# In a Mamba-2 and attention trunk, the convolved x of groups 1 to 7 is turned by VectorE in 32x32 blocks, and a DRAM scratch moves the blocks

## The chip, the cores and the metric

The kernel runs on one core of one Trainium2 chip. The metric is the device time of one launch, in microseconds; lower is better. The time before is the median of three runs, 1022.89 us (1022.04 to 1023.73).

A core has a matmul engine (TensorE, PE in the profile, with PEld for its weight loads), a vector engine (VectorE, DVE), an activation engine (ScalarE, ACT), GpSimd (POOL), and SyncE (SP), which here issues DMAs. Each engine runs its own queue of instructions in order and waits on semaphores for the others.

## What is computed

Two layers on x of 256 positions by 2048 features, float32. Layer one is a Mamba-2 SSD mixer, layer two attention in a sliding window; each is followed by a residual and a LayerNorm. The change lies in layer one. Cut to what matters, with 8 groups of 8 heads, 64 features in each head, and chunks of 128 positions:

```python
zxbcdt = x @ w_in
xbc = silu(causal_conv4(zxbcdt[..., D_INNER:D_INNER + CONV_DIM]) + conv_b)
xs, bm, cm = split(xbc)                      # xs: (256, 64 heads, 64)
x_c = xs * dt[..., None]                     # by chunk, group, head
cb = einsum("bcqgn,bcsgn->bgcqs", c_c, b_c)
y_diag = einsum("bgcqs,bgrcqs,bcsgrp->bcqgrp", cb, decay_in, x_c)
# plus the part that comes from the chunk before (y_off)
y = (y_diag + y_off) + xs * d_skip
y = y * silu(z);  y = y * rsqrt(mean(y**2) per group) * norm_w
h = y @ w_out
```

The sum over the positions s in `y_diag` needs x with positions on the partitions. The convolution works with positions along the free axis, so it leaves x the other way round: channels on the partitions. Between the two, x has to be turned.

## The kernel before

Every weight matrix comes in units of 128 x 2048 float32 (1 MB), each loaded by SP in two halves into `wr` buffers (L125, five buffers). ACT makes the rounded high half `wh` (L133) and DVE the remainder `wl` (L134); there are four slots of each. A product of full precision is three matmuls: high by high, low by high, high by low (`mac`, L195 to L197; `out_unit`, L255 to L257).

Layer one runs in 8 groups of 10 blocks. A block is one weight unit, 48 matmuls into one PSUM tile `mm` (four tiles). In groups 1 to 7 the order is B, C, four xs blocks, four z blocks (`BLOCKS`); group 0 has z first (`BLOCKS0`). After a B, C or xs block `conv_silu` empties `mm` on ACT (L357) and DVE (L359, three shifted terms) into a `cv` tile and ends with a tanh on ACT (L362) and a product on DVE (L363). After a z block, L428 and L429 do the gate. The output projection of group g-1 (`out_units`) is spread between the blocks of group g; L262 adds its result into the residual `xr`.

What else belongs to a group is placed by hand. `plan` holds, for a time counted in blocks (10 g + block), the functions that are traced after that block. For group g >= 2 the decay is loaded, summed and exponentiated first (`load_decay`, `sum_decay`, `exp_decay`), then come `cb` at 4, `tr` at 7 (`TR_AT`), `ymm` and four `gate` at 9 (`Y_AT`), and `norm` at 14. For group 0 `tr` is at 12 and `ymm` at 13, that is, inside group 1. The framework then sets each engine's queue from that order, its own estimate of when an instruction is ready and the buffers that are free, and puts in all waits. A tile's tag names the buffers that it takes turns in.

- `tr` (L453, L458): for a group, eight 128x128 transposes on PE against the identity into two PSUM tiles `ax`. DVE multiplies what came out by `dtx` (dt times a decay factor) into four tiles `xd`.
- `ymm` (L476): 32 matmuls, with `xd` as the stationary operand and the decay `e` as the moving one. DVE multiplies by `el` into `yz` (L481) and adds the skip term, which reads xs again (L487).
- `gate`: POOL multiplies by z (L492) and squares; ACT and DVE split the result into `yH` and `yL` (L506, L507) for the output projection.
- `make_dt` and `turn_dt`: once, ahead of the groups; `dtx` is made in the second (L345). The cumulated decay goes through a DRAM scratch `rscr` (stores at L327 and L330) and comes back, spread over all partitions, as `rb` (L374) and `el` (L387).

The four xs tiles of a group, the seven tiles of `make_dt` and the squares of `gate` take turns in seven buffers of 1 KB per partition with the tag `sm`.

Of the kernel before, what the change touches and what calls it, by code (L numbers as in the profile page):

```python
# [8 lines left out]
F32 = mybir.dt.float32  # L9
# [3 lines left out]
ALU = mybir.AluOpType  # L13
AX = mybir.AxisListType

P = 128
S = 256
D = 2048
KT = D // P
NG = 8  # L20
DI = 4096
KT2 = DI // P
NHD = 64
# [11 lines left out]

BLOCKS = list(range(10))
BLOCKS0 = [6, 7, 8, 9, 0, 1, 2, 3, 4, 5]
CB_AT, TR_AT, Y_AT, NSM = 4, 7, 9, 7
B_ORDER = [("q", 0), ("g", 0), ("q", 1), ("g", 1), ("o", 0), ("q", 2), ("g", 2), ("o", 1),
           ("q", 3), ("g", 3), ("o", 2), ("o", 3)]  # L40
ALPHA = (2.0 * 2) ** 0.25
# [16 lines left out]
def trunk(ctx: ExitStack, tc: tile.TileContext, A: dict, out: bass.AP, dbg=None):  # L58
    nc = tc.nc
# [12 lines left out]
    dram = pool("dram", space=bass.MemoryType.DRAM)  # L72
# [3 lines left out]
    def nm(s):  # L76
        uid[0] += 1
        return f"{s}_{uid[0]}"
# [8 lines left out]
    ident = cc[:, 0:128]  # L87
# [4 lines left out]
    pc = cst.tile([P, PC_END], F32, tag="pc", name="pc")  # L92
# [132 lines left out]
    ap = pool("ap", stack=w_stack)  # L225
# [66 lines left out]
        return pss  # L292


    dtx = ap.tile([P, 2, NHD], F32, tag="dtx", name="dtx")
    rtk = ap.tile([P, 2, 2 * NHD], F32, tag="rtk", name="rtk")
    rscr = dram.tile([P, S], F32, tag="rscr", name="rscr")

    def make_dt(ps):
        f = [ap.tile([P, S], F32, tag="sm", name=nm("f"), bufs=NSM) for _ in range(7)]  # L300
        u, e, rec, z, w, q, dt = [x[:] for x in f]
        nc.scalar.activation(u, ps[:, :S], AF.Identity, bias=pc[:, PC_DTB : PC_DTB + 1])
        nc.scalar.activation(e, u, AF.Abs)
        nc.scalar.activation(e, e, AF.Exp, scale=-1.0)
        aneg = ap.tile([P, 1], F32, tag="aneg", name="aneg")
        nc.scalar.activation(aneg[:], pc[:, PC_ALOG : PC_ALOG + 1], AF.Exp)
        nc.vector.tensor_scalar(aneg[:], aneg[:], -1.0, None, ALU.mult)
        nc.vector.tensor_scalar(rec, e, 2.0, None, ALU.add)
        nc.vector.reciprocal(rec, rec)
        nc.vector.tensor_tensor(z, e, rec, ALU.mult)  # L310
        nc.vector.tensor_tensor(w, z, z, ALU.mult)
        nc.vector.tensor_scalar(q, w, 1.0 / 15.0, None, ALU.mult)
        nc.vector.tensor_scalar(z, z, 2.0, None, ALU.mult)
        for d in (13.0, 11.0, 9.0, 7.0, 5.0, 3.0):
            nc.vector.scalar_tensor_tensor(q, q, 1.0 / d, w, ALU.add, ALU.mult)
        nc.vector.scalar_tensor_tensor(q, q, 1.0, z, ALU.add, ALU.mult)
        nc.vector.scalar_tensor_tensor(dt, u, 0.0, q, ALU.max, ALU.add)
        da, hi = e, rec
        nc.vector.tensor_scalar(da, dt, aneg[:], None, ALU.mult)
        nc.vector.tensor_scalar(hi, da, QUANT, None, ALU.add)  # L320
        nc.vector.tensor_scalar(hi, hi, QUANT, None, ALU.subtract)
        nc.vector.tensor_tensor(hi[64:128], da[64:128], hi[64:128], ALU.subtract)
        one = z
        nc.gpsimd.memset(one, 1.0)
        rc = w
        nc.vector.tensor_tensor_scan(rc, one, hi, 0.0, ALU.mult, ALU.add)
        nc.sync.dma_start(rscr[0:64, :], rc[:64])  # L327

        nc.scalar.activation(hi[64:128], rc[64:128], AF.Exp)
        nc.sync.dma_start(rscr[64:128, :], hi[64:128])  # L330
        return rc, dt, q

    def turn_dt(rc, dt, q):
        pt = ax_tile()
        for c in range(2):
            nc.tensor.transpose(pt[:, c * P : (c + 1) * P], rc[:, c * P : (c + 1) * P], ident)
            nc.tensor.transpose(
                pt[:, 256 + c * 64 : 320 + c * 64], dt[:64, c * P : (c + 1) * P], ident[:64, :64]
            )
        nc.scalar.copy(rtk[:], pt[:, :256].rearrange("p (c h) -> p c h", c=2))  # L340
        elo = q
        nc.scalar.activation(
            elo[:, :128].rearrange("p (c h) -> p c h", c=2), rtk[:, :, 64:128], AF.Exp, scale=-1.0
        )
        nc.vector.tensor_tensor(  # L345
            dtx[:], pt[:, 256:384].rearrange("p (c h) -> p c h", c=2),
            elo[:, :128].rearrange("p (c h) -> p c h", c=2), ALU.mult,
        )

    def conv_silu(ps, t, dst):  # L350
        def w(i):
            c = PC_CONV + t * 5 + i
            return pc[:, c : c + 1]

        a = ap.tile([P, S], F32, tag="cv", name=nm("cv"), bufs=3)
        with tc.high_priority(CPRI):
            nc.scalar.activation(a[:], ps[:, :S], AF.Identity, scale=w(3), bias=w(4))  # L357
            for sft in (1, 2, 3):
                nc.vector.scalar_tensor_tensor(  # L359
                    a[:, sft:], ps[:, : S - sft], w(3 - sft), a[:, sft:], ALU.mult, ALU.add  # L360
                )
        nc.scalar.activation(dst, a[:], AF.Tanh)  # L362
        nc.vector.scalar_tensor_tensor(dst, dst, 1.0, a[:], ALU.add, ALU.mult)  # L363
# [54 lines left out]
        conv_silu(ps, g * 6 + 1, gs[g].ct[:])  # L418

    def in_xs(g, i, ps):  # L420
        xs = ap.tile([P, S], F32, tag="sm", name=nm("xs"), bufs=NSM)
        conv_silu(ps, g * 6 + 2 + i, xs[:])
        gs[g].__dict__.setdefault("xs", {})[i] = xs

    def in_z(g, i, ps):
        z = ap.tile([P, S], F32, tag="zz", name=nm("z"), bufs=4)
# [16 lines left out]
            )  # L443

    def tr(g):
        st = gs[g]
        st.xd = {}
        for k in range(2):
            ps = ax_tile()
            for i in (2 * k, 2 * k + 1):  # L450
                for c in range(2):
                    o = (i % 2) * S + c * P
                    nc.tensor.transpose(ps[:, o : o + P], st.xs[i][:, c * P : (c + 1) * P], ident)  # L453
            for i in (2 * k, 2 * k + 1):
                o = (i % 2) * S
                xd = ap.tile([P, 2, 2, 64], F32, tag="xd", name=nm("xd"), bufs=4)
                hh = g * 8 + 2 * i
                nc.vector.tensor_tensor(  # L458
                    xd[:], ps[:, o : o + S].rearrange("p (c h d) -> p c h d", c=2, h=2),
                    dtx[:, :, hh : hh + 2].unsqueeze(3).to_broadcast([P, 2, 2, 64]), ALU.mult,  # L460
                )
                st.xd[i] = xd

    def ymm(g):
        st = gs[g]
        st.yz = ap.tile([P, 4, S], F32, tag="yz", name=nm("yz"), bufs=1)
        for k in range(2):
            ps = ax_tile()
            for i in (2 * k, 2 * k + 1):
                o = (i % 2) * S  # L470
                xd = st.xd[i]
                for c in range(2):
                    cols = slice(o + c * P, o + S)
                    for r in range(2):
                        e = es[g, i // 2][:, 2 * (i % 2) + r, :]
                        nc.tensor.matmul(  # L476
                            ps[64 * r : 64 * r + 64, cols], xd[:, c, r, :], e[:, 256:] if c else e[:, :256],
                            start=c == 0, stop=c == 1,
                        )
            two = slice(2 * k, 2 * k + 2)  # L480
            nc.vector.tensor_tensor(  # L481
                st.yz[:, two, :], ps[:].rearrange("p (i q) -> p i q", i=2), els[g][:, two, :], ALU.mult
            )
            for i in (2 * k, 2 * k + 1):
                col = PC_D + g * 4 + i
                v = st.yz[:, i, :]
                nc.vector.scalar_tensor_tensor(v, st.xs[i][:], pc[:, col : col + 1], v, ALU.mult, ALU.add)  # L487

    def gate(g, i):
        st = gs[g]  # L490
# [103 lines left out]
    def at(t, fn, *a):  # L594
        plan.setdefault(t, []).append((fn, *a))

    at(35, rotary)
    for g in range(NG):
        t = 10 * g
        if g == 0:  # L600
            at(TD, turn_dt, *dts)
            at(TS, load_decay, 0, 1)
            at(TS, load_low, 0)
            steps = TS
            pos = dict(cb=CB0, tr=12, y=13, norm=16)
        elif g == 1:
            at(10, load_decay, 1, 0)
            at(10, load_decay, 1, 1)
            at(13, load_low, 1)
            steps = 13  # L610
            pos = dict(cb=6, tr=TR_AT, y=Y_AT, norm=10 + CB_AT)
        else:
            at(t - 5, load_decay, g, 0)
            at(t - 5, load_decay, g, 1)
            at(t, load_low, g)
            steps = t - 1
            pos = dict(cb=CB_AT, tr=TR_AT, y=Y_AT, norm=10 + CB_AT)
        at(steps, sum_decay, g, 0)
        at(steps + 1, exp_decay, g, 0)
        at(steps + 1, sum_decay, g, 1)  # L620
        at(steps + 2, exp_decay, g, 1)
        at(t + pos["cb"], cb, g)
        at(t + pos["tr"], tr, g)
        at(t + pos["y"], ymm, g)
        for i in range(4):
            at(t + pos["y"], gate, g, i)
        at(t + pos["norm"], norm, g)
# [93 lines left out]
    for h in range(2):  # L721
        ps = mm_tile()
# [304 lines left out]
```

## Time and profile before

| | us |
|---|---|
| median of 3 runs | 1022.89 |
| lowest and highest run | 1022.04, 1023.73 |
| span of the profiled execution, first to last instruction | 1022.1 |
| PE busy in the span | 1001.7 |
| DVE busy | 774.2 |
| ACT busy | 562.8 |

For the profiled execution the page gives its span only; what lies around the span is seen from the runs, which are 0.0 to 1.6 us longer.

The page lists busy times by engine, the span in 40 slices (each digit a tenth of a slice), the DMA queues and the costliest groups of instructions. A group's row has the line, the engine, the operation, what it writes and reads, the shapes, the count, the busy time and the mean duration in ns, and after the bar the engine's idle time ahead of it, with the instruction that ended it. A row of a timeline begins with the start in us from the span's start and the duration in us; rows of the same kind in succession are merged, with their count. The windows view gives each engine's busy time in a stretch, the granted clock, the DMA share and GB/s. A row of the waits view names the waiting instruction, the one that it waited for, the time in us, the count and the longest wait.

### The profile page before, as it was taken

What the parts mean: (1) busy time and instruction counts of PE and PEld (TensorE: products, weight loads), DVE (VectorE), ACT (ScalarE), POOL (GpSimd) and SP (SyncE); (2) the same over time, 40 slices, a digit from 0 to 9 for tenths busy, and PEclk for the clock granted to TensorE, in tenths of its full rate; (3) what the DMA queues carried; (4) which work ended last, traced back from release to release, by engine and by line L of the source; (5) the groups of instructions that cost most, each with busy time, mean ns of one, the idle gap of its engine ahead of it and who ended that gap; (6) DMA issues with size and microseconds to landing.
All of it is one profiled execution on the core that took longest, in us unless ns stands there. A gap on an engine that the chain in (4) does not pass through costs nothing. (4 is left out here: it accounts for less than half of the span.)

```text
span 1022.1 us, 17627 instructions
## 1 busy us (share of the span) xinstructions
PE 1001.7 (98%) x7028; PEld 905.5 (89%) x7028; DVE 774.2 (76%) x1106; ACT 562.8 (55%) x924; POOL 89.8 (9%) x112
## 2 busy tenths in 40 slices
PE   7999999999999999999999999999999999999997
PEld 7999899999998998999999999868988879879975
DVE  6868887876886787696786787798577785785776
ACT  6585857637655655664663763535545453453642
POOL 0000303004003002100300300301000000000002
PEclk9999999999999999999999999999999999999999
DMA  8786676575666666656656556647655445545522
GB/s 308 249 299 246 204 245 195 171 233 169 211 218 191 218 195 204 205 188 202 208 179 218 156 190 210 227 146 232 197 167 169 156 140 183 173 140 183 194 96 82
DMA packets 57794, 199.31 MB, mean 195 GB/s; under 512 B 6304, under 2 KB 10672, under 8 KB 56944
## 3 DMA queue, kind: packets, MB, share of 16 engines
q1 hardware_dynamic: 56352, 192.14, 57.3%
q0 software_dynamic: 1072, 5.53, 1.5%
q8 instruction: 55, 0.90, 0.4%
q10 hardware_dynamic: 288, 0.52, 0.1%
q14 instruction: 27, 0.22, 0.1%
HBM read 195.93 MB, written 2.23 MB: 194 GB/s over the span
## 5 line engine op out<-in xcount | busy, mean ns | idle before, releaser
L134 DVE TENSOR_TENSOR wl<-wr,wh 128x1024 fp32r<-128x1024 f32 (+2 forms) x342 | 398.3, 1181 | 135.4 <-ACT wh L133 134.0
L133 ACT ACTIVATE wh<-wr 128x1024 fp32r<-128x1024 f32 (+2 forms) x342 | 337.4, 1011 | 238.9 <-PE mm L196 77.1
L195 PE MATMUL mm<-xH,wh 128*128 128x256 f32 x1296 | 361.2, 279 | 8.0 <-ACT wh L153 6.0
L197 PE MATMUL mm<-xH,wl 128*128 128x256 f32 x1296 | 359.8, 278 | 2.1 <-DVE wl L134 2.1
L196 PE MATMUL mm<-xL,wh 128*128 128x256 f32 x1296 | 360.1, 278 | 0.0
L195 PEld LDWEIGHTS mm<-xH,wh 128*128 128x128 f32 x1296 | 244.6, 189 | 10.2 <-ACT wh L153 6.3
L197 PEld LDWEIGHTS mm<-xH,wl 128*128 128x128 f32 x1296 | 244.5, 189 | 2.7 <-DVE wl L134 2.7
L196 PEld LDWEIGHTS mm<-xL,wh 128*128 128x128 f32 x1296 | 244.7, 189 | 1.1
L255 PE MATMUL mm<-wh,yH 128*128 128x512 f32 x256 | 101.4, 396 | 0.0
L256 PE MATMUL mm<-wh,yL 128*128 128x512 f32 x256 | 99.9, 390 | 0.0
L257 PE MATMUL mm<-wl,yH 128*128 128x512 f32 x256 | 99.7, 390 | 0.0
L492 POOL TENSOR_TENSOR yz<-yz,z 128x256 f32<-128x256 f32 x32 | 32.9, 1036 | 532.0 <-DVE yz L487 532.0
L195 PE MATMUL mm<-x1H,wh 128*128 128x256 f32 x256 | 71.9, 281 | 0.0
L197 PE MATMUL mm<-x1H,wl 128*128 128x256 f32 x256 | 71.0, 277 | 0.0
L196 PE MATMUL mm<-x1L,wh 128*128 128x256 f32 x256 | 71.0, 277 | 0.0
L359 DVE SCALAR_TENSOR_TENSOR cv<-mm,pc,cv 128x255 f32<-128x255 f32 x144 | 68.6, 476 | 1.4
L712 PE MATMUL mm<-wh,x1H 128*128 128x512 f32 x160 | 63.3, 396 | 0.0
L714 PE MATMUL mm<-wl,x1H 128*128 128x512 f32 x160 | 62.6, 392 | 0.3 <-DVE wl L134 0.2
L713 PE MATMUL mm<-wh,x1L 128*128 128x512 f32 x160 | 62.6, 391 | 0.2 <-DVE x1L L676 0.2
L255 PEld LDWEIGHTS mm<-wh,yH 128*128 128x128 f32 x256 | 48.1, 188 | 10.3 <-DVE z L429 1.0
L257 PEld LDWEIGHTS mm<-wl,yH 128*128 128x128 f32 x256 | 48.1, 188 | 10.2
L256 PEld LDWEIGHTS mm<-wh,yL 128*128 128x128 f32 x256 | 48.1, 188 | 9.0
(180 smaller groups left out, 1306.2 us busy)
## 6 DMA issues: line engine op xcount, KB each, us to landing
wr<-in_wa SPq DMA_DIRECT2D x158, 512.0 KB, 5.0
wr<-in_wo SPq DMA_DIRECT2D x64, 512.0 KB, 4.8
wr<-in_wq SPq DMA_DIRECT2D x32, 512.0 KB, 4.5
wr<-in_wg SPq DMA_DIRECT2D x32, 512.0 KB, 5.2
wr<-in_wb SPq DMA_DIRECT2D x32, 512.0 KB, 4.6
rb<-rscr SPq DMA_DIRECT2D x16, 512.0 KB, 5.4
el<-rscr SPq DMA_DIRECT2D x16, 256.0 KB, 4.8
wr<-in_wkv SPq DMA_DIRECT2D x8, 512.0 KB, 4.3
```

Of the source, the lines that this page charges most:

```text
L133: nc.scalar.activation(h[:, sl], raw, AF.Copy)
L134: nc.vector.tensor_tensor(l[:, sl], raw, h[:, sl].bitcast(F32), ALU.subtract)
L195: nc.tensor.matmul(ps, ah, bh, start=first, stop=False)
L196: nc.tensor.matmul(ps, ah, bl, start=False, stop=False)
L197: nc.tensor.matmul(ps, al, bh, start=False, stop=last)
L255: nc.tensor.matmul(ps[:], aH[:, k, hs], u.h[:, ks], start=k == 0, stop=False)
L256: nc.tensor.matmul(ps[:], aL[:, k, hs], u.h[:, ks], start=False, stop=False)
L257: nc.tensor.matmul(ps[:], aH[:, k, hs], u.l[:, ks], start=False, stop=k == 3)
L359: nc.vector.scalar_tensor_tensor(a[:, sft:], ps[:, : S - sft], w(3 - sft), a[:, sft:], ALU.mult, ALU.add)
L712: nc.tensor.matmul(ps[:], x1H[:, kk, hs], u.h[:, ks], start=kk == 0, stop=False)
L713: nc.tensor.matmul(ps[:], x1L[:, kk, hs], u.h[:, ks], start=False, stop=False)
L714: nc.tensor.matmul(ps[:], x1H[:, kk, hs], u.l[:, ks], start=False, stop=kk == KT - 1)
```

## The change

In groups 1 to 7 `tr` is replaced by three steps:

- `turn_blocks`, after block 5: two VectorE transposes, one for each chunk, turn every 32x32 block of the group's x in place of the whole 128x128. The result `zt` has the positions within a block of 32 on the partitions. Four stores on SP, one for each band of 32 partitions, write it to a DRAM scratch `zd` so that the blocks stand in the order that a whole transpose would give.
- `load_turned`, after block 6: one load on SP brings it back as `xt`, with all 128 positions on the partitions.
- `scale_x`, after block 8: two DVE multiplications by `dtx` of 512 columns each, from SBUF, give `xd`.

`ymm` stays after block 9. Group 0 keeps `tr` with PE and the identity.

Buffers change along with it. A group's four xs are one tile with the tag `xs` and one buffer; four of the seven tiles of `make_dt` use that buffer before. The tag `sm` goes from seven buffers to three. `xd` is one tile for a group, and `zt` and `xt` take turns with `yz` in its one buffer. `dtx` is laid out by group, and is written by two instructions in place of one.

```diff
-CB_AT, TR_AT, Y_AT, NSM = 4, 7, 9, 7
+CB_AT, ZT_AT, LD_AT, XD_AT, Y_AT, NSM = 4, 5, 6, 8, 9, 3
...
-    dtx = ap.tile([P, 2, NHD], F32, tag="dtx", name="dtx")
+    dtx = ap.tile([P, NG, 2, 8], F32, tag="dtx", name="dtx")
...
     def make_dt(ps):
-        f = [ap.tile([P, S], F32, tag="sm", name=nm("f"), bufs=NSM) for _ in range(7)]
-        u, e, rec, z, w, q, dt = [x[:] for x in f]
+        f = [ap.tile([P, S], F32, tag="sm", name=nm("f"), bufs=NSM) for _ in range(3)]
+        f4 = ap.tile([P, 4, S], F32, tag="xs", name=nm("f4"), bufs=1)
+        u, e, rec, z = [f4[:, i, :] for i in range(4)]
+        w, q, dt = [x[:] for x in f]
...
-        nc.vector.tensor_tensor(
-            dtx[:], pt[:, 256:384].rearrange("p (c h) -> p c h", c=2),
-            elo[:, :128].rearrange("p (c h) -> p c h", c=2), ALU.mult,
-        )
+        for c in range(2):
+            cols = slice(64 * c, 64 * c + 64)
+            nc.vector.tensor_tensor(
+                dtx[:, :, :, 4 * c : 4 * c + 4],
+                pt[:, 256:384][:, cols].rearrange("p (g i r) -> p g r i", i=4, r=2),
+                elo[:, cols].rearrange("p (g i r) -> p g r i", i=4, r=2), ALU.mult,
+            )
...
     def in_xs(g, i, ps):
-        xs = ap.tile([P, S], F32, tag="sm", name=nm("xs"), bufs=NSM)
-        conv_silu(ps, g * 6 + 2 + i, xs[:])
-        gs[g].__dict__.setdefault("xs", {})[i] = xs
+        if i == 0:
+            gs[g].xs = ap.tile([P, 4, S], F32, tag="xs", name=nm("xs"), bufs=1)
+        conv_silu(ps, g * 6 + 2 + i, gs[g].xs[:, i, :])
...
     def tr(g):
         st = gs[g]
-        st.xd = {}
+        st.xd = ap.tile([P, 8, 2, 64], F32, tag="xd", name=nm("xd"), bufs=1)
...
+    def turn_blocks(g):
+
+        st = gs[g]
+        zt = ap.tile([P, 4, 2, 4, 32], F32, tag="yz", name=nm("zt"), bufs=1)
+        xv = st.xs[:].rearrange("p i (c b t) -> p c b i t", c=2, b=4)
+        for c in range(2):
+            nc.vector.transpose(zt[:, :, c, :, :], xv[:, c, :, :, :])
+        st.zd = dram.tile([4, P, 256], F32, tag="zd", name=nm("zd"), bufs=2)
+        for a in range(4):
+            nc.sync.dma_start(
+                st.zd[a, :, :].rearrange("(b t) f -> t b f", b=4),
+                zt[32 * a : 32 * a + 32, :, :, :, :].rearrange("p b c i d -> p b (c i d)"),
+            )
+
+    def load_turned(g):
+        st = gs[g]
+        st.xt = ap.tile([P, 2, 2, 8, 32], F32, tag="yz", name=nm("xt"), bufs=1)
+        nc.sync.dma_start(st.xt[:].rearrange("p r a k d -> p (r a) (k d)"), st.zd[:].rearrange("a p f -> p a f"))
+
+    def scale_x(g):
+
+        st = gs[g]
+        st.xd = ap.tile([P, 8, 2, 64], F32, tag="xd", name=nm("xd"), bufs=1)
+        xv = st.xd[:].rearrange("p k r (a d) -> p r a k d", a=2)
+        for r in range(2):
+            nc.vector.tensor_tensor(
+                xv[:, r, :, :, :], st.xt[:, r, :, :, :],
+                dtx[:, g, r, :].unsqueeze(1).unsqueeze(3).to_broadcast([P, 2, 8, 32]), ALU.mult,
+            )
...
-                            ps[64 * r : 64 * r + 64, cols], xd[:, c, r, :], e[:, 256:] if c else e[:, :256],
+                            ps[64 * r : 64 * r + 64, cols], st.xd[:, 4 * c + i, r, :], e[:, 256:] if c else e[:, :256],
...
-        at(t + pos["tr"], tr, g)
+        if g == 0:
+            at(t + pos["tr"], tr, g)
+        else:
+            at(t + pos["zt"], turn_blocks, g)
+            at(t + pos["ld"], load_turned, g)
+            at(t + pos["xd"], scale_x, g)
```

In `tr` the two multiplications per PSUM tile now take one chunk of both i each, in place of both chunks of one i.

More of the change, by code (lines that the diff above doesn't have):

```diff
@@ L452, in tr @@
                     o = (i % 2) * S + c * P
[L453 to L457, printed above, removed]
+                    nc.tensor.transpose(ps[:, o : o + P], st.xs[:, i, c * P : (c + 1) * P], ident)
+            for c in range(2):
+                two = slice(4 * c + 2 * k, 4 * c + 2 * k + 2)
                 nc.vector.tensor_tensor(
-                    xd[:], ps[:, o : o + S].rearrange("p (c h d) -> p c h d", c=2, h=2),
-                    dtx[:, :, hh : hh + 2].unsqueeze(3).to_broadcast([P, 2, 2, 64]), ALU.mult,
-                )
-                st.xd[i] = xd
+                    st.xd[:, two, :, :],
+                    ps[:].rearrange("p (i c r d) -> p c i r d", i=2, c=2, r=2)[:, c, :, :, :],
+                    dtx[:, g, :, two].rearrange("p r i -> p i r").unsqueeze(3).to_broadcast([P, 2, 2, 64]),
+                    ALU.mult,
+                )
+    def turn_blocks(g):
+        st = gs[g]
+        zt = ap.tile([P, 4, 2, 4, 32], F32, tag="yz", name=nm("zt"), bufs=1)
+        xv = st.xs[:].rearrange("p i (c b t) -> p c b i t", c=2, b=4)
+        for c in range(2):
+            nc.vector.transpose(zt[:, :, c, :, :], xv[:, c, :, :, :])
[18 more added lines that the diff above has]
+            )
     def ymm(g):
@@ L470, in ymm @@
                 o = (i % 2) * S
-                xd = st.xd[i]
                 for c in range(2):
@@ L486, in ymm @@
                 v = st.yz[:, i, :]
-                nc.vector.scalar_tensor_tensor(v, st.xs[i][:], pc[:, col : col + 1], v, ALU.mult, ALU.add)
+                nc.vector.scalar_tensor_tensor(v, st.xs[:, i, :], pc[:, col : col + 1], v, ALU.mult, ALU.add)
     def gate(g, i):
@@ L610, in trunk @@
             steps = 13
-            pos = dict(cb=6, tr=TR_AT, y=Y_AT, norm=10 + CB_AT)
+            pos = dict(cb=6, zt=ZT_AT, ld=LD_AT, xd=XD_AT, y=Y_AT, norm=10 + CB_AT)
         else:
@@ L616, in trunk @@
             steps = t - 1
-            pos = dict(cb=CB_AT, tr=TR_AT, y=Y_AT, norm=10 + CB_AT)
+            pos = dict(cb=CB_AT, zt=ZT_AT, ld=LD_AT, xd=XD_AT, y=Y_AT, norm=10 + CB_AT)
         at(steps, sum_decay, g, 0)
```

## The prediction

> **What bounds the kernel now.** I read the page's first two parts, then the windows by stage, then the waits of the stage that changes, and only then single instructions.
>
> ```profile
> span 1022.1 us, 17627 instructions
> PE 1001.7 (98%) x7028; PEld 905.5 (89%) x7028; DVE 774.2 (76%) x1106; ACT 562.8 (55%) x924; POOL 89.8 (9%) x112
> PEclk9999999999999999999999999999999999999999
> ```
>
> TensorE (PE) is busy for 98% of the span, at full granted clock in every slice. The next engine, VectorE (DVE), has 76%. A busy PE in these records need not be PE at its peak, so the stage itself must be looked at. The windows view (us, PE, PEld, DVE, ACT, POOL busy, clock, DMA share, GB/s) and the waits view of PE from 130 to 640 us give:
>
> ```profile
> 350.00:410.00 60.00, 60.00 (x439) 55.26 (x438) 47.24 (x62) 32.47 (x47) 6.42 (x8) 1.00 0.62 200
> 640.00:700.00 60.00, 57.31 (x263) 45.57 (x262) 53.19 (x70) 28.19 (x37) 7.98 (x13) 1.00 0.54 183
> ```
> ```profile
> PE mm L195 <- DVE cv L359: 0.6, 1, 0.6
> ```
>
> The reader is to see that in the stretch of the SSD groups PE has no idle time to speak of: 60.00 of 60, and one wait of 0.6 us in 510 us. An instruction taken out of PE's queue there shortens the run by the time until the next one starts. The second window is the step between the two layers, where DVE and PE hand over to each other; the change touches nothing there, it only comes earlier.
>
> Is what feeds PE ahead of it? The waits view from 170 to 640 us answers:
>
> ```profile
> ACT wh L133 <- PE mm L196: 48.8, 18, 4.1
> ```
>
> ScalarE (ACT), which makes the high half of each weight unit, waits 48.8 us for PE to give a `wh` slot back. The weights stand ready as far ahead as four slots allow, so PE can go faster by a per cent and find them.
>
> **The change part by part.**
>
> *Removed from PE.* In groups 1 to 7 the eight transposes of `tr` go. Their price is not their duration. The PE timeline of group 3 and the line view of L453 show both:
>
> ```profile
> 300.24 0.28 PE L197 MATMUL mm<-xH,wl 128*128 128x256 f32 x1
> 300.35 1.04 PE L453 MATMUL ax<-cc,xs 128*128 128x128 f32 x8
> 301.14 0.36 PE L195 MATMUL mm<-xH,wh 128*128 128x256 f32 x1
> 301.34 0.28 PE L196 MATMUL mm<-xL,wh 128*128 128x256 f32 x1
> 301.46 0.28 PE L197 MATMUL mm<-xH,wl 128*128 128x256 f32 x1
> ```
> ```profile
> L453 PE MATMUL ax<-cc,xs x64: 270/272/273, 91.8 to 616.0; 128*128 128x128 f32 x64
> ```
>
> One transpose is recorded with 272 ns, but matmuls overlap: eight of them cover 300.35 to 301.14, some 0.1 us each. From the L197 at 300.24 to the L196 at 301.34 are 1.10 us. Without the transposes two steps of an ordinary matmul would stand there, and such a step is 0.11 to 0.12 us (300.24 to 300.35, 301.34 to 301.46). So a batch costs 1.10 - 0.23 = 0.87 us. Seven batches: **-6.1 us**. Group 0 keeps its eight.
>
> Beside this the Trainium skill, page "TensorE: Matmul & The Clock Gate", section "Part 4: PE-mode transpose", gives about 275 ns for a transpose inside a kernel. Taken as the price, that would be 56 x 0.275 = 15.4 us, an estimate from that page. The record's 272 ns agrees with it as a duration; the step of 0.1 us between starts speaks against it as a price.
>
> *DVE.* Removed are four `xd` multiplications per group; added are two block transposes and two multiplications of 128x512 each. Rows by form, from 130 to 640 us, and the windows view of DVE alone:
>
> ```profile
> L441 DVE TENSOR_TENSOR e<-e,cbm 128x1536 f32<-128x1536 f32 x12 | 21.0, 1747 | 0.0
> L458 DVE TENSOR_TENSOR xd<-ax,dtx 128x256 f32<-128x256 f32 x28 | 10.4, 417 | 11.5 <-PE ax L453 11.5
> L481 DVE TENSOR_TENSOR yz<-ax,el 128x512 f32<-128x512 f32 x14 | 9.0, 680 | 0.0
> ```
> ```profile
> 100.00:130.00 30.00, 27.39 (x37) 1.00 0.64 200
> 130.00:640.00 510.00, 390.81 (x522) 1.00 0.62 200
> ```
>
> No block transpose is in this trace. Its bounds: 0.42 us, as the `xd` operation of half the columns, and 1.75 us, as the operation of three times the columns. I take 0.7, since L481 has the same 512 columns. Multiplications: 0.68 each, from the same row. Per group 4 x 0.68 - 4 x 0.417 = +1.05 us, at the ends +0.5 and +3.2. DVE has 119 us idle in those 510 us, some 23%, so 7 us in all (3.5 to 22) lie in its gaps: 0 on the path. In return DVE loses its waits for the transposes (11.5 us in L458's row). The second `dtx` multiplication of group 0's preparation is one more small DVE instruction, at most the 0.42 us of an `xd` operation, before the groups; I take 0.
>
> *The way through DRAM.* New are four stores and one load on SP's queue per group, a DVE instruction that waits for the load, and PE's `ymm` behind it. It has to fit between the last convolved x and `ymm`. Group 3, DVE's and then PE's timeline:
>
> ```profile
> 292.91 0.43 DVE L363 SCALAR_TENSOR_TENSOR xs<-xs,cv 128x256 f32<-128x256 f32 x1 [0.54 <-ACT xs L362]
> 300.99 0.76 DVE L458 TENSOR_TENSOR xd<-ax,dtx 128x256 f32<-128x256 f32 x2 [0.85 <-PE ax L453]
> 307.91 1.23 DVE L134 TENSOR_TENSOR wl<-wr,wh 128x1024 fp32r<-128x1024 f32 x1 [2.76 <-ACT wh L133]
> 318.78 1.22 DVE L134 TENSOR_TENSOR wl<-wr,wh 128x1024 fp32r<-128x1024 f32 x1 [3.21 <-ACT wh L133]
> ```
> ```profile
> 317.69 2.82 PE L476 MATMUL ax<-e,xd 128*64 128x256 f32 x32
> ```
> The tile view of `rscr`, the one scratch that already goes through DRAM (issues, then all landings), the page's DMA issues, and the SP queue's own waits:
> ```profile
> L327 SPq DMA_DIRECT2D rscr<-f x1: 523/523/523, 46.2 to 46.2; - x1
> DMA to landing us min/median/max: 2.0/5.0/8.0
> ```
> ```profile
> rb<-rscr SPq DMA_DIRECT2D x16, 512.0 KB, 5.4
> ```
> ```profile
> SPq L125 <- DVE wl L134: 636.9, 270, 12.7
> ```
>
> x is complete at 293.3. One weight split of 1.2 may stand ahead, two block transposes take 1.4: 295.9. Four issues of 0.52 take 2.1, landing 5.0 (median of the `rscr` transfers): 303.0. The load takes 0.5 to issue and 5.4 to land: 308.9. Scaling, 1.4: 310.3. `ymm` would begin at 317.69 - 0.87 = 316.8, so **6.5 us are to spare**, and the cost is 0. What can use this up is SP's queue. It is in order and a weight load in it waits for its `wr` slot, on average 636.9 / 270 = 2.4 us, at most 12.7. A store or load that arrives behind one waits with it. Two average waits leave 1.7 us.
>
> Behind the waiting instructions: on SP the later weight loads, for whom ACT waits; the `wh` row says that they are early. On DVE behind the scaling stand weight splits and the emptying of `mm`; the idle times of 2.76 and 3.21 us shown above lie in this very stretch and cover a wait of that size. The new traffic, 1 MB per group, is little beside the 200 GB/s x 60 us = 12 MB of the window 350 to 410 shown above.
>
> *One buffer for x.* The four xs tiles of a group now share one buffer, and so do two groups. From group 1 on the next group's x comes long after `ymm` has read the old one. At group 0 it does not, since its `tr` and `ymm` are placed at 12 and 13, inside group 1. ACT, DVE and PE there:
>
> ```profile
> 101.74 0.42 ACT L362 ACTIVATE xs<-cv 128x256 f32<-128x256 f32 x1 [1.91 <-DVE cv L359]
> 103.46 1.05 ACT L133 ACTIVATE wh<-wr 128x1024 fp32r<-128x1024 f32 x1
> 117.42 1.04 ACT L133 ACTIVATE wh<-wr 128x1024 fp32r<-128x1024 f32 x1
> ```
> ```profile
> 108.62 1.71 DVE L487 SCALAR_TENSOR_TENSOR yz<-xs,pc,yz 128x256 f32<-128x256 f32 x2
> ```
> ```profile
> 125.63 0.35 PE L195 MATMUL mm<-xH,wh 128*128 128x256 f32 x1 [1.32 <-DVE cv L359]
> ```
>
> Group 1's first tanh into xs runs at 101.74; it must now wait until group 0's last L487 has read xs, at 110.3: 8.6 us later. Behind it on ACT stand `wh` splits, the emptying of `mm` and the decay. If all of it reached PE, it would cost 8.6; if the reshuffle removed the wait of 1.32 shown, it would gain 1.3. I take 0: ACT makes no split between 103.46 and 117.42 today, and PE's wait behind that hole is for L359, not for weights.
>
> **Sum.** -6.1 + 0 + 0 + 0: span 1016.0. The median of the runs is 0.8 above the profiled span (1022.89 against 1022.1), so **1016.8 us**.
>
> **The rivals.**
>
> *A stall at group 0's hand-over eats part of the gain.* For: DVE is busy 27.39 of 30 us there, and PE already waits once. Against: the ACT hole above. I price it at a third of the 8.6, 2.9 us: 1019.7. Chance 0.14.
>
> *VectorE waits in its queue for the load.* Scaling sits in order ahead of weight splits and `mm` drains. Up to the two idle times, 6 us, nothing shows; a wait about 0.9 us above that costs PE as much as the transposes did: 1022.9. For: loads land in anything from 2.0 to 8.0 us. Against: the splits run far ahead. Chance 0.12.
>
> *The turned blocks come late for `ymm`*, the case on the other side. PE would then stand before L476 in each of seven groups. It decides from 6.5 us added to the chain above (PE starts to wait) and makes the kernel slower from 7.4. With both landings at 8.0 (+5.6), transposes at 1.75 (+2.1) and an average slot wait on SP for store and load (+4.8) the chain is 12.5 longer: 6.0 us late, x7 = 42 us, so 1059; one microsecond past that gives 1016.8 + 7 x 1.9 = 1030. For: each step has such a row. Against: they would have to come together in every group. Chance 0.12. The Trainium skill, page "VectorE: DVE Perf Modes", section "Rules for kernel authors", also speaks against the change: for 128x128 it advises TensorE where PSUM is an acceptable destination. No row here shows the detour's cost, so I leave that rule the chance of this rival.
>
> *PE is freed of the full recorded duration.* If each transpose blocked PE for 272 ns, 56 x 0.272 = 15.2 us would go: 1007.7. The step between starts contradicts it. Chance 0.02. (This is what the skill's 275 ns would mean.)
>
> **How the numbers follow.** My forecast has chance 0.60; its own range is 1014.3 to 1018.5: 1.3 and 0.6 lower if PE's two named waits go too and the runs scatter (1022.04 to 1023.73), 1.7 higher for small losses at the hand-over. The range reaches on to the hand-over rival and most of the DVE rival: 1014.3 to 1022.6, which leaves out the late blocks, the full-duration case and a little of the rest. Faster by over 0.2% (2 us, about what a measurement of this kernel tells from no change): 0.60 + 0.14 + 0.02 = 0.76; within it 0.12; slower 0.12.
>
> **What would show it.** In the changed profile L453 should have 8 PE transposes, not 64, and group 3's `ymm` should come some 0.9 us per earlier group sooner. PE should have no wait before L476 named after the scaling, and the windows of the groups should still read 60.00 of 60. The block transposes should read near 0.7 us. The load should land some 7 us before `ymm`. ACT may show a wait before L362 near 102 to 110 us; if PE then shows one of several microseconds near 110 to 130, the hand-over rival holds. The forecast is wrong if PE waits in each group, or if PE's stream has its steps lengthened so that the freed time does not appear.

## The result, and the profile after

| | before | changed | ratio, 95% interval |
|---|---|---|---|
| first measurement, median (lowest to highest) | 1022.75 (1022.04 to 1023.73) | 1017.46 (1016.0 to 1018.88) | 0.9949 [0.9935, 0.9963] |
| again, beside the later experiments | 1022.62 (1021.36 to 1025.15) | 1016.45 (1014.29 to 1019.42) | 0.9938 [0.9922, 0.9954] |
| span of the first profile | 1022.1 | 1017.1 | |

The change saves 5.3 and 6.2 us in the two measurements; the forecast was 1016.8 us, some 6 less. Of all runs below one, of ten with group 0 on VectorE too, took 2572.57 us; no trace shows why, and the ratios leave it out. The page of the changed kernel, its span, busy times and costliest line of PE, reads:

```profile
span 1017.1 us, 17576 instructions
PE 998.2 (98%) x6972; PEld 900.9 (89%) x6972; DVE 781.5 (77%) x1107; ACT 563.8 (55%) x924; POOL 89.9 (9%) x112
L195 PE MATMUL mm<-xH,wh 128*128 128x256 f32 x1296 | 361.2, 279 | 7.9 <-ACT wh L153 6.1
```

PE still has 98% of a shorter span, with 56 instructions fewer (7028 to 6972), and an ordinary matmul takes the 279 ns that it took. DVE's busy time grew by 7.3 us; what of that reached PE is worked out behind the experiments. PE's stream of transposes and `ymm`, from the line and tile views of the changed kernel:

```profile
L459 PE MATMUL ax<-cc,xs x8: 272/272/273, 93.2 to 94.0; 128*128 128x128 f32 x8
L510 PE MATMUL ax<-e,xd x256: 272/326/430, 99.6 to 629.9; 128*64 128x256 f32 x64, 128*64 128x128 f32 x64
```

The second row is the handle for what follows: from group 0's first `ymm` to group 7's last lie all seven groups that changed, and neither the start of the kernel nor the attention layer. Of the kernel before, the same row is

```profile
L476 PE MATMUL ax<-e,xd x256: 272/326/431, 98.3 to 635.1; 128*64 128x256 f32 x64, 128*64 128x128 f32 x64
```

The stretch shrank from 536.8 to 530.3 us, by 6.5. The windows view of that stretch (us, PE, PEld, DVE, ACT, POOL busy, clock, DMA share, GB/s), before and changed:

```profile
98.30:635.10 536.80, 534.88 (x4134) 503.48 (x4136) 415.28 (x556) 318.62 (x480) 67.15 (x79) 1.00 0.63 201
```
```profile
99.60:629.90 530.30, 528.94 (x4081) 497.50 (x4080) 422.52 (x557) 319.24 (x480) 67.20 (x79) 1.00 0.68 217
```

PE was busy for 5.9 us less and stood still for 0.6 us less, at the same clock. Yet group 0's `ymm` came 1.3 us later. That is no work of the change: in the second profile of the changed kernel it stands at 95.9, and the stretch is 530.5.

```profile
L510 PE MATMUL ax<-e,xd x256: 272/326/430, 95.9 to 626.4; 128*64 128x256 f32 x64, 128*64 128x128 f32 x64
```

So between two profiles of one kernel the start differs by 3.7 us and the stretch by 0.2. Inside the stretch, one group's step can be seen in the timelines of PE. First before, then changed, `ymm` of groups 3 and 4:

```profile
317.69 2.82 PE L476 MATMUL ax<-e,xd 128*64 128x256 f32 x32
...
399.13 2.82 PE L476 MATMUL ax<-e,xd 128*64 128x256 f32 x32
```
```profile
315.90 2.39 PE L510 MATMUL ax<-e,xd 128*64 128x256 f32 x26
...
396.48 2.71 PE L510 MATMUL ax<-e,xd 128*64 128x256 f32 x30
```

81.44 us became 80.58: 0.86 for one group, against 0.87 worked out. (The shorter durations and counts of the last two rows are those of the windows that were asked for.)

The way of the turned blocks, in the tile views of `zt` and `xt` (durations in ns least/median/most, first and last start, then landings or waits):

```profile
L475 DVE STREAM_TRANSPOSE zt<-xs x14: 668/688/712, 127.1 to 611.7; 128x512 f32<-128x512 f32 x14
...
DMA to landing us min/median/max: 3.2/3.8/6.0
```
```profile
L494 DVE TENSOR_TENSOR xd<-xt,dtx x14: 678/683/693, 142.1 to 625.1; 128x512 f32<-128x512 f32 x14
...
  DMA xt<-zd: 1.3, 3
...
DMA to landing us min/median/max: 4.6/5.4/6.7
```

A block transpose takes 0.69 us, a store lands in 3.8, the load in 5.4, and DVE waited for a load in three of seven groups, 1.3 us altogether. PE never waited for one. Its waits from 130 to 640 us, changed kernel:

```profile
PE mm L195 <- DVE cv L364: 0.8, 1, 0.8
PE mm L255 <- DVE xr L262: 0.5, 1, 0.5
```

The first is the wait of 0.6 from before, at the same place. The second is new, at 133.8 us. The wait of 1.32 us at 125.63 is gone.

### The profile page after: what moved, and what is told of

Its sections match the earlier page's. It is cut to its first block, busy times and chain, and to the rows that moved or that the text cites. A ratio compares the mean times of both kernels' runs of the same rounds, so it can differ in the third digit from the quotient of the medians.

```text
span 1017.1 us, 17576 instructions
## 1 busy us (share of the span) xinstructions
PE 998.2 (98%) x6972; PEld 900.9 (89%) x6972; DVE 781.5 (77%) x1107; ACT 563.8 (55%) x924; POOL 89.9 (9%) x112
## 4 chain that ended last, share of the span: by engine, by line
PE 76%; DVE 10%; DMA 5%; ACT 4%; issue 3%; POOL 1%; SPq 0%; DVEq 0%; ACTq 0%; POOLq 0%
PE mm L195 13%; PE mm L196 13%; PE mm L197 13%; PE mm L255 7%; PE mm L256 7%; PE mm L257 7%; PE mm L751 3%; PE mm L752 3%; PE mm L753 3%; DVE wl L134 3%; DMA wr<-in_wa 3%; ACT wh L133 2%; DVE cv L364 1%; DMA wr<-in_wo 1%; PE ax L510 1%
## 5 line engine op out<-in xcount | busy, mean ns | idle before, releaser
L364 DVE SCALAR_TENSOR_TENSOR cv<-mm,pc,cv 128x255 f32<-128x255 f32 x144 | 68.6, 477 | 2.0 <-ACT cv L362 0.6
```

The lines of the kernel that those rows point to most:

```text
L364: nc.vector.scalar_tensor_tensor(a[:, sft:], ps[:, : S - sft], w(3 - sft), a[:, sft:], ALU.mult, ALU.add)
```

## The experiments

The theory: the gain is what eight transposes take in PE's stream, 0.87 us, seven times; all that replaces them lies beside PE. Three other answers were open: that the rearranged buffers made part of the gain, that PE did not pay for the transposes what the steps between starts say, and that the detour costs something that a larger saving hides. Each run is compared with the kernel before on the same chip: 1023.62 us for the buffers alone, the transposes twice, the second trip and group 0 on VectorE at the old place of its `ymm`; 1022.62 for the others.

### The buffers alone

```diff
-        if g == 0:
-            at(t + pos["tr"], tr, g)
...
+        if True:
+            at(t + pos.get("tr", 7), tr, g)
```

> All buffer and layout edits of the change stay (one buffer for x, three buffers sm, one xd, dtx by group), but groups 1 to 7 turn on PE again (tr at 7). Theory (the gain is PE's eight transposes per group, 0.87 us a batch; buffers cost nothing): back at the kernel before, 1022.7 us within 1 us, and group 1's ymm no earlier than 153.5 us. Rival (the one buffer for x costs at group 0's hand-over): 1 to 3 us above the kernel before, with PE waits between 100 and 135 us. Rival (the buffers bring a part of the gain): 1018 to 1021.

Measured: 1022.57 us, ratio 0.9991 [0.998, 1.0002], which doesn't tell a microsecond from none. The trace tells more; the tile view's row of `ymm`:

```profile
L510 PE MATMUL ax<-e,xd x256: 272/326/431, 96.8 to 631.9; 128*64 128x256 f32 x64, 128*64 128x128 f32 x64
```

The stretch is 535.1 us, 1.7 less than before, and PE has no wait between 90 and 140 us. So there is no cost at group 0's hand-over, but a small gain, about the size of the wait of 1.32 us that went. This was not expected: group 1's `ymm` was to come no earlier than 153.5 us and came at 150.86, 54.11 us after group 0's, where the kernel before has 55.68. Of the 6.5 us of the whole change three quarters are missing without the transposes' removal. How the wait goes is seen in DVE's timeline where it empties the `mm` of group 1's last x block, before and then in the changed kernel:

```profile
121.96 0.47 DVE L359 SCALAR_TENSOR_TENSOR cv<-mm,pc,cv 128x255 f32<-128x255 f32 x1
122.36 1.21 DVE L134 TENSOR_TENSOR wl<-wr,wh 128x1024 fp32r<-128x1024 f32 x1
123.49 0.47 DVE L359 SCALAR_TENSOR_TENSOR cv<-mm,pc,cv 128x254 f32<-128x254 f32 x1
123.88 1.21 DVE L134 TENSOR_TENSOR wl<-wr,wh 128x1024 fp32r<-128x1024 f32 x1
125.01 0.47 DVE L359 SCALAR_TENSOR_TENSOR cv<-mm,pc,cv 128x253 f32<-128x253 f32 x1
```
```profile
122.01 1.00 DVE L364 SCALAR_TENSOR_TENSOR cv<-mm,pc,cv 128x255 f32<-128x255 f32 x2 [0.61 <-ACT cv L362]
122.96 1.23 DVE L134 TENSOR_TENSOR wl<-wr,wh 128x1024 fp32r<-128x1024 f32 x1
124.10 0.47 DVE L364 SCALAR_TENSOR_TENSOR cv<-mm,pc,cv 128x253 f32<-128x253 f32 x1
```

Three steps of the convolution stood with two weight splits between them, now with one. The queue is laid out anew around the later x of group 1, and the last of the three steps ends at 124.57 in place of 125.48. That the one buffer for x caused this order, and not another of the edits kept here, wasn't taken apart.

### The transposes twice, in the kernel before

```diff
-                for c in range(2):
+                for c in [0, 0, 1, 1] if g else range(2):
                     o = (i % 2) * S + c * P
                     nc.tensor.transpose(ps[:, o : o + P], st.xs[i][:, c * P : (c + 1) * P], ident)
```

> The kernel before with every transpose of groups 1 to 7 issued twice into the same place: 56 more. Theory (a batch of eight in the stream costs 0.87 us, later ones 8 x 0.109): +6.1 us, 1028.8. Rival (each blocks PE for its recorded 272 ns): +15.2, 1037.9. Rival (PE has slack at these places, so the gain of the change came from elsewhere): 1022.7.

Measured: 1029.47 us, ratio 1.0058 [1.0044, 1.0072], that is +5.9 us (+4.5 to +7.4). The stretch:

```profile
L476 PE MATMUL ax<-e,xd x256: 272/326/430, 97.5 to 639.7; 128*64 128x256 f32 x64, 128*64 128x128 f32 x64
```

542.2 us, 5.4 more; the wait near 124 us was 0.6 shorter in this run, so 6.0 belong to the 56 transposes, 0.107 us each. From group 3 to group 6, where PE waits for nothing, a step from `ymm` to `ymm` grew from 81.44 to 82.32. A recorded duration of 272 ns that overlaps its neighbours is not a price. Both rivals fall.

### Without the way through DRAM

```diff
-        st.zd = dram.tile([4, P, 256], F32, tag="zd", name=nm("zd"), bufs=2)
-        for a in range(4):
-            nc.sync.dma_start(
...
+        st.xt = zt[:].rearrange("p (r a) c i d -> p r a (c i) d", r=2)
```

> Leaves out the way through DRAM: scaling reads what the block transposes wrote, so the blocks stand in the wrong places. Everything else as in the changed kernel. Theory (stores, load and the waits that they bring lie beside PE's stream): same time as the changed kernel run beside it, within 1 us. Rival (SP's waits for the blocks and the 1 MB per group slow the weights and with them PE): 2 to 5 us below the changed kernel.

Measured: 1016.4 us, 0.9938 [0.9925, 0.9952], beside 1016.45 for the changed kernel. In the times the detour of 1 MB per group, SP's waits and the load cost nothing that can be told. The trace has a little; the row of `ymm`:

```profile
L503 PE MATMUL ax<-e,xd x256: 272/326/430, 96.9 to 626.7; 128*64 128x256 f32 x64, 128*64 128x128 f32 x64
```

The stretch is 529.8 us, against 530.3 and 530.5 in the two profiles of the changed kernel, so the detour costs about half a microsecond, not far above the difference between these two.

### A second trip through DRAM

```diff
+        back = dram.tile([P, 1024], F32, tag="zd2", name=nm("zd2"), bufs=2)
+        nc.sync.dma_start(back[:], st.xt[:].rearrange("p r a k d -> p (r a k d)"))
+        st.xt = ap.tile([P, 2, 2, 8, 32], F32, tag="yz", name=nm("xt"), bufs=1)
+        nc.sync.dma_start(st.xt[:].rearrange("p r a k d -> p (r a k d)"), back[:])
```

> The turned x goes through DRAM a second time (one store and one load of 512 KB more per group), some 9 to 10 us longer. In the changed kernel xd is ready 9.6 to 11.4 us ahead of ymm in groups 1 to 6, and 1.6 us ahead in group 7. Theory (only what is longer than this spare time costs): groups 1 to 6 cost 0 to 1 us together, group 7 up to 8 us, less where its ymm, which now stands 28 matmuls later in PE's queue, finds other work ahead: 1018 to 1026. Rival (each transfer on SP's queue costs through the weight loads): 10 us and more, spread evenly over the groups.

Measured: 1018.34 us, 0.9952 [0.9937, 0.9968]: no slower than the changed kernel can be told. In groups 1 to 6 `xd` was now ready only 0.9 to 2.1 us ahead of `ymm`. PE's waits from 130 to 640 us in this kernel:

```profile
PE mm L195 <- DVE cv L364: 1.0, 2, 0.7
PE ax L514 <- DVE xd L498: 0.5, 1, 0.5
PE mm L255 <- DVE xr L262: 0.2, 1, 0.2
```

One wait for `xd`, of 0.5 us, in group 7, although there the chain was over 6 us too long for the old place: the planner had put that `ymm` 28 matmuls further back. Behind it PE had a new wait of 1.2 us, for `sq` at 646.48, while waits of 1.9 us for `xr` soon after shrank to 0.3. From group 0's `ymm` to the end are 918.7 us, against 917.5 and 918.0 in the changed kernel, so the second trip cost about 1 us, the lower end of the expectation.

### Group 0 on VectorE too

```diff
-            pos = dict(cb=CB0, tr=12, y=13, norm=16)
+            pos = dict(cb=CB0, zt=9, ld=10, xd=12, y=13, norm=16)
```

> Group 0 too turns on VectorE (blocks at 9, load at 10, scaling at 12, ymm at 13 as before). Its x is complete near 88.5 us and its ymm stands near 99 us, 11 us later, where a group's chain from x to xd took 12.6 to 18 us. Theory (late blocks stop PE): PE waits 3 to 8 us before group 0's ymm, 0.9 us come back from the transposes, so 1019.5 to 1024.5. Rival (other PE work or slack hides it): 1016.6.

Measured: 1022.49 us (1022.26 without the run of 2572.57), 0.9986 [0.9977, 0.9996]: of the gain of 0.5 to 0.6% little is left. PE's timeline:

```profile
97.68 0.28 PE L195 MATMUL mm<-xH,wh 128*128 128x256 f32 x1
103.06 3.13 PE L510 MATMUL ax<-e,xd 128*64 128x256 f32 x15 [5.10 <-DVE xd L494]
```

PE stands 5.10 us for `xd`. Here is the rival of the late blocks, in the one group where the time from x to `ymm` is too short, and one such wait takes back nearly six batches of transposes. x was complete at 88.7 us, and `ymm` would have begun at 97.96, 9.2 later; the chain took 14.9, to 103.6.

### The block transposes four times

```diff
-            nc.vector.transpose(zt[:, :, c, :, :], xv[:, c, :, :, :])
+            for _ in range(4):
+                nc.vector.transpose(zt[:, :, c, :, :], xv[:, c, :, :, :])
```

> Each block transpose is issued four times into the same place: 6 x 0.69 = 4.1 us more of VectorE per group, 29 us in all, where VectorE is idle for 108 of 510 us. Theory (VectorE's idle time takes it): same as the changed kernel, within 1 us; at most PE's wait near 282 us grows. Rival (VectorE is near its limit where the groups meet, its totals hide this): 3 to 15 us more, as waits of PE for L364 or L262 in each group.

Measured: 1019.01 us, 0.9959 [0.9946, 0.9972], 2.6 us above the changed kernel beside it: a miss. The two intervals overlap, but the stretch shows it too: it is 533.6 us long, 3.1 to 3.3 more than in the two profiles of the changed kernel. PE's waits in the same view as above, and the windows of DVE in the changed kernel and then in this one:

```profile
PE mm L195 <- DVE cv L364: 2.0, 2, 1.4
PE mm L197 <- DVE wl L134: 0.6, 1, 0.6
PE mm L195 <- DVE xr L262: 0.5, 1, 0.5
PE ax L511 <- DVE xd L495: 0.2, 1, 0.2
```
```profile
100.00:130.00 30.00, 27.93 (x41) 1.00 0.65 195
...
290.00:640.00 350.00, 272.35 (x355) 1.00 0.67 214
```
```profile
100.00:130.00 30.00, 27.93 (x42) 1.00 0.62 195
...
290.00:640.00 350.00, 288.80 (x384) 1.00 0.66 214
```

From 290 us on, 16.45 us more of DVE work cost one wait of 0.2 us. The rest lies at 134, 201 and 282 us, in groups 1 to 3. How group 1 falls behind is seen in the timelines of DVE, SP and ACT, changed kernel and then this one:

```profile
129.09 1.20 DVE L134 TENSOR_TENSOR wl<-wr,wh 128x1024 fp32r<-128x1024 f32 x1
130.86 0.42 SPq L125 DMA_DIRECT2D wr<-in_wa  x1
133.31 1.06 ACT L133 ACTIVATE wh<-wr 128x1024 fp32r<-128x1024 f32 x1 [0.86 <-DMA wr<-in_wa]
```
```profile
125.23 3.65 DVE L476 STREAM_TRANSPOSE zt<-xs 128x512 f32<-128x512 f32 x6
133.90 4.61 DVE L134 TENSOR_TENSOR wl<-wr,wh 128x1024 fp32r<-128x1024 f32 x4
135.17 0.35 SPq L125 DMA_DIRECT2D wr<-in_wa  x1
139.12 1.06 ACT L133 ACTIVATE wh<-wr 128x1024 fp32r<-128x1024 f32 x1 [8.79 <-DMA wr<-in_wa]
```

DVE has hardly a gap there, so the extra transposes push the next weight split from 129.09 to 133.90. The split frees a weight buffer, the next load goes out at 135.17 in place of 130.86, and ACT stands 8.79 us for weights. PE's new wait of 0.6 us for `wl`, at 135.16, is for the first of these late splits. The delay is still there in group 2: counted from group 0's `ymm`, its first convolution step (L364) comes 4.6 us later than in the changed kernel (78.97 against 74.40), although DVE is busy for only 22.02 of 30 us from 160 to 190 in both. DVE and ACT wait for each other in turn there, 5.15 us a block, where PE takes 5.47, so only 0.3 us a block is made up. That this delay is also what PE waits for at 201 us is read from the trace; no run tests it. So DVE's idle total does not tell what more work costs.

### Group 0 on VectorE, its `ymm` one block later

```diff
-OUT_AT = [[], [6, 7, 8, 9]] + [[4, 6, 8, 9]] * 5 + [[7]]
+OUT_AT = [[], [7, 8, 9]] + [[4, 6, 8, 9]] * 5 + [[7]]
...
-            pos = dict(cb=CB0, tr=12, y=13, norm=16)
+            pos = dict(cb=CB0, zt=9, ld=10, xd=12, y=14, norm=17)
```

> Group 0 turns on VectorE, and its ymm comes one block later (14, norm 17), the first output unit of group 0 after block 7 of group 1 in place of 6. A block is 5.5 us, and PE waited 5.1 us for xd when group 0 turned on VectorE with ymm at 13. Theory: that wait goes, the eight transposes give 0.9 us, so 0.5 to 1.2 us below the changed kernel. Rival (group 1's x, which waits for group 0's ymm to free the one buffer, comes later and takes it back): 0 to 4 us above the changed kernel, with PE waits between 110 and 160 us.

Measured: 1015.39 us, 0.9928 [0.9915, 0.9941], with no wait of PE between 90 and 160 us. It is the fastest median of all, 1.06 below the changed kernel beside it (0.9938 [0.9922, 0.9954]). The intervals overlap, so that it beats the changed kernel is likely and not shown; that it beats the kernel before is.

### The changed kernel again

> The changed kernel itself, on the same chip as the three runs beside it. Theory: 0.9945 of the kernel before, some 5.5 us less. PE's waits of 0.5 to 0.8 us near 134 and 282 us again, and the first group's start anywhere within 3 us of the earlier run (profiles so far have it from 13.8 to 16.4 us).

Measured: 1016.45 us, given with the result above. The wait near 282 us was 1.06 in this run.

## Why the prediction was right, and where its steps were off

The starts of `ymm` in the PE timelines give one step per group, in us; the last column is from group 0's first to group 7's first.

| | 0 to 1 | 1 to 2 | 2 to 3 | 3 to 4 | 4 to 5 | 5 to 6 | 6 to 7 | all |
|---|---|---|---|---|---|---|---|---|
| before | 55.68 | 81.44 | 82.24 | 81.44 | 81.44 | 81.44 | 70.57 | 534.25 |
| changed | 54.06 | 80.58 | 81.64 | 80.58 | 80.58 | 80.58 | 69.67 | 527.69 |
| changed, second profile | 54.10 | 80.59 | 81.86 | 80.58 | 80.58 | 80.58 | 69.67 | 527.96 |
| buffers alone | 54.11 | 81.44 | 82.20 | 81.44 | 81.44 | 81.44 | 70.56 | 532.63 |
| transposes twice | 55.95 | 82.31 | 83.01 | 82.32 | 82.31 | 82.32 | 71.43 | 539.65 |
| without the way through DRAM | 53.75 | 80.58 | 81.53 | 80.58 | 80.58 | 80.58 | 69.68 | 527.28 |
| block transposes four times | 55.01 | 82.26 | 81.37 | 80.58 | 80.58 | 80.58 | 70.15 | 530.53 |

So seven batches take 6.0 us out of PE's stream and the buffers 1.6; VectorE's new work gives back some 0.7 and the way through DRAM 0.4 to 0.7. The last two are near the 0.3 by which two profiles of one kernel differ. The forecast had 6.1, 0, 0 and 0: the main term was right, and the three that were put at nothing cancel to within 0.6. That they do is luck.

- **PE is the bound, and a batch costs 0.87 us.** Shown in three ways: 0.86 to 0.90 in each step without a wait, 5.9 us less of PE's busy time in the stretch of the seven groups (the other 0.6 of the 6.5 is the vanished wait of 1.3, less 0.5 and 0.2 of other waits), and +5.9 us when they are issued twice. The price by recorded duration, the last rival, would have given 1007.7.
- **VectorE's part is hidden.** All but about 0.7 us of it. Sizes were met: 0.69 for a block transpose (0.7 taken), 0.68 for the scaling. The sum was +1.05 a group, 7.35 in seven; the page has 7.3 more. But without the way through DRAM and with the same buffers, the seven steps shrink by 5.4 us (532.63 to 527.28), not by the transposes' 6.0: PE has a new wait of 0.2 for `xr` in group 1, and its wait near 282 us grows from 0.5 to 0.7. The argument, 119 us of idle time in 510, was too generous: with 4.1 us more per group the idle time is still there and 2.6 us are lost. It nearly held because the true sum was small.
- **The way through DRAM fits, with 6.5 us to spare.** PE never waits for `xd` in the changed kernel, so the conclusion was right, and the size was off in both directions. SP and then DVE of the changed kernel in group 3:

```profile
293.82 1.86 SPq L478 DMA_DIRECT2D zd<-zt  x4
295.78 0.40 SPq L125 DMA_DIRECT2D wr<-in_wo  x1
296.39 0.35 SPq L125 DMA_DIRECT2D wr<-in_wa  x1
298.58 0.38 SPq L486 DMA_DIRECT2D xt<-zd  x1
```
```profile
292.49 1.31 DVE L475 STREAM_TRANSPOSE zt<-xs 128x512 f32<-128x512 f32 x2
...
303.74 1.29 DVE L494 TENSOR_TENSOR xd<-xt,dtx 128x512 f32<-128x512 f32 x2 [0.45 <-DMA xt<-zd]
```

  The stores are issued as the second block transpose ends, and the load 2.9 us after the last store's issue: the two weight loads between them took 0.4 us each to issue and held nothing up, and a store landed in 3.8 where 5.0 were taken. `xd` was ready at 305.0 and `ymm` began at 315.9, so 10.9 were to spare. But group 3 was taken for all seven. In group 7 one output unit stands among the blocks, so `ymm` is nearer to x. DVE and PE of the changed kernel there:

```profile
624.45 1.28 DVE L494 TENSOR_TENSOR xd<-xt,dtx 128x512 f32<-128x512 f32 x2
```
```profile
627.31 2.82 PE L510 MATMUL ax<-e,xd 128*64 128x256 f32 x32
```

  1.6 us were to spare. The trace of before could have said so: its last x and last `ymm` are 18.2 us apart, in group 3 it is 24.4. By the forecast's own sum, 17.0 from x to `xd`, and with 0.9 for the transposes, group 7 had only 0.3 to spare, not 6.5. And the price that the rival of the late blocks set, seven times the lateness, left out that the planner can move `ymm` back, as it did in the second-trip run; where it doesn't, as in group 0, the lateness is paid in full.
- **The hand-over at group 0 costs 0.** The delay came, with the first tanh into xs at 111.18 in place of 101.74, and reached no wait of PE. The edits to the buffers gave a little instead: the wait of 1.32 us went. This was one end of the bounds and not the value taken. The rival there (1019.7) does not show in any run.
- **DVE waiting in its queue for the load.** It happened, for 1.3 us in all (4.2 in the second profile), and PE waited for none of it by name.
- **The sum.** The median is 0.7 above the forecast in one measurement and 0.35 below in the other. The start of the kernel alone moves by more. The 0.8 us from span to median is not what lies around the span, as the text ahead of the forecast has it: every run that lists its own span takes 1.7 to 2.1 us longer than that (1018.88 against 1017.1). The profiled execution of the kernel before was therefore about 1 us slower than the median; the sum is not touched by this.

## What to carry to other kernels

Price an instruction on the bounding engine by the steps between starts with it and without it, not by its recorded duration. A detour of 13 to 18 us cost some 0.7 us at most, in all seven groups, where the consumer came 17 to 28 us later in the other engine's queue, and most of the gain where it came after 9: measure that distance in every iteration, the first and the last above all. Idle time of a helper engine in total is no proof of room: ask what stands behind the new work in its queue, here the weight split that lets the next load go out.

## What the runs showed of the hardware that was not expected

A block transpose of 128x512 float32 on VectorE took 0.69 us, the same as a multiplication of that size (0.68), so turning 32x32 blocks cost no more than a pass over the data. Stores of 128 KB from 32 partitions landed in 3.8 us at the median, the load of 512 KB in 5.4, while the core's DMA moved 215 GB/s (130 to 640 us). These are not constants: in the run with the block transposes four times the same stores landed in 2.3 us and the load in 6.9. And two profiles of one kernel put group 0's `ymm` at 95.9 and 99.6 us, while the seven groups after it took 530.5 and 530.3, and their steps without a wait agreed to 0.01 us.
